# The combinations for the seven-product form: made in small steps on plain weight tiles, apart from the transposes

## Chip, core and metric

One core of a Trainium2 chip runs the whole kernel in one launch. The metric is device time in microseconds (us), the median of several executions.

## What is computed

A two-layer decoder trunk over 256 tokens of 2048 channels, float32. Layer 0 is a diagonal state-space mixer with a gated output, layer 1 an attention layer; each is followed by the same feed-forward block, which takes most of the time:

```python
def swiglu(u, w_gate, w_up, w_down):
    return (jax.nn.silu(u @ w_gate) * (u @ w_up)) @ w_down
...
u = rmsnorm(h, g_ffn[i])
h = h + swiglu(u, w_gate[i], w_up[i], w_down[i])      # D_MODEL 2048, D_FF 5632
```

## The kernel before

Every float32 operand of a matmul is split into a rounded part hi and a rest lo, and a product is three matmuls (hi by hi, lo by hi, hi by lo). The weights stream from HBM in tiles of 512 by 512, 1 MB each; a job is the use of one tile by TensorE (PE). `jobs` is a list, and the order of everything around it is written out by hand: `run_stream` (line 148) walks the list, and for job i it issues the matmuls, then the splits of the tiles ahead (`split_ahead`, line 121), then the functions that were hung behind job i (`j.after`, filled from `pend`). A split is `hi` on ScalarE (ACT, line 113) and `lo = raw - hi` on VectorE (DVE, line 114), in units of two blocks (128x1024); a full tile has two units. The hi and lo buffers hold four units, so a new split waits until PE has left the unit that it overwrites. DVE and ACT each work in the order of issue: what is hung behind job i stands in both queues between the split of job i+1 and that of job i+2.

A plain tile is 4 blocks by 2 token halves by 3 matmuls, 24 matmuls of 512 columns. The feed-forward block goes over D_FF in eleven groups of 512 columns, in two halves (groups 0 to 5, then 6 to 10); after each half comes the down product of that half. Groups after the first use a seven-product (Strassen-like) form for one 2x2 corner of the product: seven small tiles of 6 matmuls each and six plain tiles, 13 jobs in this order: small 1, 6, 7, plain, small 5, plain, small 2, 3, 4, and four plain tiles (jobs 9 to 12). Four of the small products need combinations of the weights (`S_T1` to `S_T4`, lines 786 to 789, on DVE; those for a group are made behind jobs 10 and 11 of the group before) and combinations of u. The down products use the same form, with combinations of g.

The combinations of u, `SC["c"]`, are made once per layer by `s_combine` (line 187). It stands in `u_chunk` (line 641) in the place of the transposing routine `hT_blocks` for the first 4 of 16 channel blocks: it transposes those blocks with PE, scales them, splits them, and forms, splits and stores the combinations, for two block pairs b = 0 and 1, all behind one job. In layer 0 this is a job of the gated output (the glu product), in layer 1 a job of the w_o product. The other 12 blocks go through `hT_blocks` (line 171) at later jobs.

The combinations of g, `SC["g"]`, are made once per half by `g_combine` (line 872). `g_rows` (line 858) transposes a finished group of g on PE into a PSUM bank `tr`, one token half a at a time, behind jobs 2 and 3 of the next group, splits it, and for the first two groups of a half calls `g_combine` at once: n = 0 (one copy) and n = 1 (copy, difference, split) in the second group, n = 2 (nothing) and n = 3 in the third. `g_combine` with n = 3 is one chain on DVE and ACT: five combining operations on DVE and three splits, each an ACT copy and a DVE subtraction, 128x512 each.

In the same group `s_evac` (line 813) empties the PSUM banks: behind job 9 two silus on ACT and one subtraction on DVE, behind job 12 four operations on DVE, which give the g that `g_rows` transposes in the next group.

Of the kernel before, what the change touches and what calls it, by code (L numbers as in the profile page):

```python
# [9 lines left out]
F32 = mybir.dt.float32  # L10
F32R = mybir.dt.float32r
AF = mybir.ActivationFunctionType
OP = mybir.AluOpType
# [17 lines left out]
def trunk_kernel(ctx: ExitStack, tc: tile.TileContext, par, x_tok, x_grp, b_st, g_st, c_st, cst, gvec,  # L31
# [24 lines left out]
    def bank(tag):  # L56
        return ps.tile([128, 512], F32, name=f"{tag}_{bank.n()}", tag=tag, bufs=2 if tag in ("tr", "x") else 1)
# [15 lines left out]
    def add(src, t, mm, after=None):  # L73
        j = Job()
        j.src, j.t, j.mm, j.after, j.pre = src, t, mm, after or [], []
        j.part, j.make, j.home = None, None, None
        jobs.append(j)
        return j
# [105 lines left out]

    SC = {}

    def s_combine(un, g):

        t = big.tile([128, 4096], F32R, name=f"sc_{un}", tag="DA"[un == "u_f1"])
        q = big.tile([128, 2, 2, 4, 128], F32R, name=f"sq_{un}", tag="Q")  # L190
        SC["c"] = t[:, 0:2048].rearrange("p (s n b t) -> p s n b t", s=2, n=4, b=2)
        SC["g"] = [q, t[:, 2048:4096].rearrange("p (s n b t) -> p s n b t", s=2, n=2, b=4)]
        SC["x"] = [big.tile([128, 512], F32, name=f"sx{n}_{un}", tag=f"X{n}") for n in range(2)]
        for b in range(2):
            tr = bank("tr").rearrange("p (b a t) -> p b a t", b=2, a=2)
            X = rows.tile([128, 2, 2, 128], F32, name=f"X{b}_{un}", tag="row")
            V = rows.tile([128, 4, 128], F32, name=f"V{b}_{un}", tag="row")
            for bb in range(2):
                for a in range(2):
                    k = b + 2 * bb  # L200
                    pe.transpose(tr[:, bb, a], h[:, a, 128 * k:128 * k + 128], ident)
            for bb in range(2):
                k = b + 2 * bb
                x = X[:, bb].rearrange("p a t -> p (a t)")
                act.activation(X[:, bb], tr[:, bb], AF.Copy, scale=g[:, k:k + 1])
                act.activation(uT[un][:, 0, k], x, AF.Copy)
                dve.tensor_tensor(uT[un][:, 1, k], x, uT[un][:, 0, k], op=OP.subtract)
            dve.tensor_tensor(V[:, 2], X[:, 0, 1], X[:, 0, 0], op=OP.subtract)
            dve.tensor_tensor(V[:, 0], X[:, 0, 1], X[:, 1, 1], op=OP.subtract)
            dve.tensor_tensor(V[:, 1], X[:, 1, 1], V[:, 2], op=OP.subtract)  # L210
            dve.tensor_tensor(V[:, 3], X[:, 1, 0], V[:, 1], op=OP.subtract)
            act.activation(SC["c"][:, 0, :, b], V, AF.Copy)
            dve.tensor_tensor(SC["c"][:, 1, :, b], V, SC["c"][:, 0, :, b], op=OP.subtract)


    pt = ring.tile([128, 32, 64], F32, name="gam", tag="hi")
# [409 lines left out]
    def row():  # L626
        return rows.tile([128, 512], F32, name=f"row{bank.n()}", tag="row")
# [13 lines left out]
    def u_chunk(j, c, name, gs):  # L641
        def f():
            if c == 0:
                u_tile(name)
            if c == 0 and name != "u_kv":
                s_combine(name, gv[:, gs])
            else:
                hT_blocks(range(4 * c, 4 * c + 4), uT[name], gv[:, gs])
        pend.append((j, f))

    PS = {}
# [105 lines left out]
    def gu_job(nm, un, own, kg, first, last, joins=None):  # L757
        o = opnd1(lambda: uT[un])

        def f(j):  # L760
            if joins is None and first:
                gu_acc(nm, own)
            mm3(acc[nm], o, 4 * kg, j, first, last, joins=joins or ())
        return f
# [93 lines left out]
    def g_rows(l, hf, c, src, a):  # L858
        def f():
            t = src()  # L860
            tr = bank(NT[a]).rearrange("p (b t) -> p b t", b=4)
            for b in range(4):
                pe.transpose(tr[:, b], t[:, 128 * b:128 * b + 128], ident)
            dst, b0 = g_at(l, hf, 4 * (c - PARTS[hf][0]))
            ts = slice(128 * a, 128 * a + 128)
            act.activation(dst[:, 0, b0:b0 + 4, ts], tr, AF.Copy)
            dve.tensor_tensor(dst[:, 1, b0:b0 + 4, ts], tr, dst[:, 0, b0:b0 + 4, ts], op=OP.subtract)
            if c - PARTS[hf][0] < 2:
                g_combine(2 * (c - PARTS[hf][0]) + a, tr, dst[:, :, b0:b0 + 4])
        return f  # L870

    def g_combine(n, tr, g):

        v4 = lambda t: t.rearrange("p (b t) -> p b t", b=4)
        X0, X1 = [v4(t) for t in SC["x"]]

        def put(i, src):
            d = SC["g"][i // 2]
            act.activation(d[:, 0, i % 2], src, AF.Copy)
            dve.tensor_tensor(d[:, 1, i % 2], src, d[:, 0, i % 2], op=OP.subtract)  # L880

        if n == 0:
            act.activation(X0, tr, AF.Copy)
        if n == 1:
            act.activation(X1, tr, AF.Copy)
            dve.tensor_tensor(X0, tr, X0, op=OP.subtract)
            put(2, X0)
        if n == 3:
            V = v4(row())
            dve.tensor_tensor(X1, X1, tr, op=OP.subtract)  # L890
            put(0, X1)
            dve.tensor_tensor(V, tr, X0, op=OP.subtract)
            put(1, V)
            t0 = slice(0, 128)
            dve.tensor_tensor(X0, g[:, 0, :, t0].bitcast(F32), V, op=OP.subtract)
            dve.tensor_tensor(X0, X0, g[:, 1, :, t0].bitcast(F32), op=OP.add)
            put(3, X0)


    def d_load(l, hf, cp, wd):  # L900
# [114 lines left out]
    def ffn(l, un, wg, wu, wd, r, down_evac):  # L1015
        for hf, (ca, cb) in enumerate(PARTS):
            for c in range(ca, cb):
                own = (c + 1) % 2
                j0 = len(jobs)
                if c == 0:  # L1020
                    for nm, w in (("gate", wg), ("up", wu)):
                        for kg in range(4):
                            add(w, 4 * c + kg, gu_job(nm, un, own, kg, kg == 0, kg == 3))
                    pend.append((j0 + 4, gate_evac(c, r)))
                    pend.append((j0 + 7, gu_end))
                    pend.append((j0 + 8, up_evac(c)))
                    src = lambda a, c=c: (lambda: sil[c][a])
                else:
                    pend.append((j0 - 5, s_load(l, c, wg, wu)))
                    pend.append((j0 - 3, S_T1))  # L1030
                    pend.append((j0 - 2, S_T2))
                    pend.append((j0 - 2, S_T3))
                    X = lambda nm, w, kg: add(w, 4 * c + kg, gu_job(nm, un, own, kg, kg == 1, kg == 3, (0,) if nm == "gate" else (0, 1)))
                    for i in (1, 6, 7):
                        s_add(i, un, own)
                    X("gate", wg, 1)
                    s_add(5, un, own)
                    X("gate", wg, 2)
                    for i in (2, 3, 4):
                        s_add(i, un, own)  # L1040
                    X("gate", wg, 3)
                    for kg in (1, 2, 3):
                        X("up", wu, kg)
                    for n in (0, 1, 2, 4, 9, 12):
                        pend.append((j0 + n, s_evac(n, c, r)))
                    src = lambda a, c=c: (lambda: gr[c, a])
                e = len(jobs) + (2 if c + 1 < cb else 0)
                for a in range(2):
                    pend.append((e + a, g_rows(l, hf, c, src(a), a)))
            k0, k1 = ca, cb  # L1050
            for cp in range(2):
                if l == 1 and hf == 1 and cp == 1:
                    for c in (2, 3):
                        for kg in range(k0, k1):
                            add(wd, 11 * c + kg, mm_job(("down", l, hf, c), kg == k0, kg == k1 - 1, g_opnd(l, hf), 4 * (kg - k0)))
                        chunk_end(len(jobs), down_evac(c))
                    continue
                down_pair(l, hf, cp, wd, (cp + hf + 1) % 2, r)
                n = len(jobs)
                for i in range(2):  # L1060
                    c = 2 * cp + i
                    if hf == 0:
                        chunk_end(n - 1 + i, lambda c=c: add_hr(("down", l, 0, c), c, r))
                    else:
                        chunk_end(n - 1 + i, down_evac(c))
                        if l == 0:
                            u_chunk(n + 1 + i, c, "u_kv", 0)
# [430 lines left out]
```

## Time and profile before

| | us |
|---|---|
| median of 3 executions | 2116.58 |
| lowest and highest | 2113.69, 2120.05 |
| the profiled execution, its own time | 2113.41 |
| its span in the trace | 2111.3 |
| PE busy in it | 2058.3 (97%) |
| DVE busy | 1548.0 (73%) |
| ACT busy | 1054.6 (50%) |
| POOL (GpSimd) busy | 150.9 (7%) |

The span is the time from the first to the last instruction in the trace. Busy shares are averages over the whole span; what ends a wait in a stretch is read from the timeline of that stretch. A matmul's recorded end is modelled and lies after the start of the next one, so the distance from start to start tells more of PE's pace than its busy time.

### The profile page before, as it was taken

Reading aid. Unit: us, or ns where it says so; the run is one execution under the profiler, and the core shown is the slowest. Engines: PE = TensorE matmul, PEld = TensorE weight load, DVE = VectorE, ACT = ScalarE, POOL = GpSimd, SP = SyncE. Lnnn points to the kernel's source line nnn. Section 1 sums busy time; section 2 is a strip of 40 time slices with the busy share of each in tenths; the row PEclk is TensorE's granted clock in tenths of the full one; section 3 lists DMA queues with packets and bytes.
Section 4 is the critical chain, followed back from the end, with each engine's and each line's share of the span. In section 5 each row is a group of like instructions: output and inputs, shape, how many; then the busy total and the mean of one; then the engine's idle time right before and its main releaser. Section 6 shows DMA issues by size and latency. Waiting matters only on the chain.

```text
span 2111.3 us, 28945 instructions
## 1 busy us (share of the span) xinstructions
PE 2058.3 (97%) x11508; PEld 1720.3 (81%) x11508; DVE 1548.0 (73%) x2124; ACT 1054.6 (50%) x1326; POOL 150.9 (7%) x105
## 2 busy tenths in 40 slices
PE   7999999999999999999999999999999999999998
PEld 6778787888888778888999998787788888778886
DVE  8984867777887777787555555667777878777784
ACT  6344555544554545555444444555455554544553
POOL 7741400000000000000000000000000000000010
PEclk9999999999999999999999999999999999999999
DMA  3035555555545455554544544555465456545544
GB/s 141 25 121 154 184 199 187 212 200 191 216 174 216 160 178 181 199 199 160 176 164 162 179 162 165 175 215 174 173 215 198 157 200 241 197 168 191 199 170 149
DMA packets 54055, 376.20 MB, mean 178 GB/s; under 512 B 6432, under 2 KB 6944, under 8 KB 9120
## 3 DMA queue, kind: packets, MB, share of 16 engines
q1 hardware_dynamic: 53920, 374.36, 49.7%
q8 instruction: 90, 1.47, 0.3%
q14 instruction: 45, 0.37, 0.1%
HBM read 370.14 MB, written 2.10 MB: 176 GB/s over the span
## 4 chain that ended last, share of the span: by engine, by line
PE 80%; DVE 12%; ACT 4%; issue 3%; DMA 0%; SPq 0%; ACTq 0%; POOL 0%; POOLq 0%; DVEq 0%
PE acc L139 12%; PE acc L138 12%; PE acc L137 12%; DVE lo L114 5%; PE tr L139 4%; PE tr L137 4%; PE tr L138 4%; PE x L138 3%; PE x L137 3%; PE x L139 3%; PE acc L1106 3%; PE acc L1107 3%; PE acc L1105 3%; ACT hi L113 3%; PE acc L146 2%
## 5 line engine op out<-in xcount | busy, mean ns | idle before, releaser
L114 DVE TENSOR_TENSOR lo<-raw,hi 128x1024 fp32r<-128x1024 f32 x552 | 666.9, 1242 | 202.8 <-ACT hi L113 199.3
L113 ACT ACTIVATE hi<-raw 128x1024 fp32r<-128x1024 f32 x566 | 575.9, 1053 | 200.0 <-PE acc L138 107.8
L137 PE MATMUL acc<-hi,u_f 128*128 128x512 f32 x608 | 238.0, 392 | 0.6 <-ACT hi L113 0.5
L139 PE MATMUL acc<-lo,u_f 128*128 128x512 f32 x608 | 237.2, 390 | 0.7 <-DVE lo L114 0.7
L138 PE MATMUL acc<-hi,u_f 128*128 128x512 f32 x608 | 237.0, 390 | 0.0
L139 PEld LDWEIGHTS acc<-lo,u_f 128*128 128x128 f32 x608 | 114.2, 188 | 25.4 <-DVE lo L114 1.6
L137 PEld LDWEIGHTS acc<-hi,u_f 128*128 128x128 f32 x608 | 114.2, 188 | 24.4 <-ACT hi L113 0.9
L138 PEld LDWEIGHTS acc<-hi,u_f 128*128 128x128 f32 x608 | 114.2, 188 | 23.8 <-DVE u_f L182 0.3
L113 ACT ACTIVATE hi<-st 128x1024 fp32r<-128x1024 f32 x60 | 63.3, 1056 | 115.2 <-DVE st L783 111.9
L139 PE MATMUL acc<-lo,g 128*128 128x512 f32 x256 | 99.9, 390 | 0.5 <-DVE lo L114 0.5
L137 PE MATMUL acc<-hi,g 128*128 128x512 f32 x256 | 100.0, 391 | 0.0
L138 PE MATMUL acc<-hi,g 128*128 128x512 f32 x256 | 99.7, 390 | 0.0
L137 PE MATMUL x<-hi,u_f 128*128 128x512 f32 x240 | 94.4, 393 | 0.0
L139 PE MATMUL x<-lo,u_f 128*128 128x512 f32 x240 | 93.6, 390 | 0.0
L138 PE MATMUL x<-hi,u_f 128*128 128x512 f32 x240 | 93.5, 390 | 0.0
L137 PE MATMUL tr<-hi,u_f 128*128 128x512 f32 x240 | 93.5, 389 | 0.0
L139 PE MATMUL tr<-lo,u_f 128*128 128x512 f32 x240 | 93.5, 389 | 0.0
L138 PE MATMUL tr<-hi,u_f 128*128 128x512 f32 x240 | 93.5, 389 | 0.0
L114 DVE TENSOR_TENSOR lo<-st,hi 128x1024 fp32r<-128x1024 f32 x60 | 73.3, 1222 | 25.6 <-ACT hi L113 24.1
L164 POOL TENSOR_TENSOR sml<-sml,half 128x2 f32<-128x2 f32 x4 | 2.8, 700 | 1121.7 <-DVE sml L163 1121.6
L1105 PE MATMUL acc<-uq,hi 128*128 128x256 f32 x256 | 74.0, 289 | 0.0
L1105 PE MATMUL acc<-u_kv,hi 128*128 128x256 f32 x256 | 73.3, 287 | 0.1
(375 smaller groups left out, 4806.4 us busy)
## 6 DMA issues: line engine op xcount, KB each, us to landing
raw<-w_gate SPq DMA_DIRECT2D x68, 1024.0 KB, 5.0
raw<-w_up SPq DMA_DIRECT2D x68, 1024.0 KB, 4.9
raw<-w_down SPq DMA_DIRECT2D x67, 1024.0 KB, 5.0
raw<-w_kv SPq DMA_DIRECT2D x32, 1024.0 KB, 4.9
su<-w_up SPq DMA_DIRECT2D x20, 1024.0 KB, 4.8
sg<-w_gate SPq DMA_DIRECT2D x20, 1024.0 KB, 7.1
raw<-w_glu SPq DMA_DIRECT2D x16, 1024.0 KB, 5.0
raw<-w_q SPq DMA_DIRECT2D x16, 1024.0 KB, 4.8
```

The source lines that it names most:

```text
L113: act.activation(hi, raw, AF.Copy)
L114: (pool if i < NPRE else dve).tensor_tensor(lo, raw, hi, op=OP.subtract)
L137: pe.matmul(pr, oh, j.hi[kb], start=first and kb == 0 and not jn, stop=False, skip_group_check=jn)
L138: pe.matmul(pr, ol, j.hi[kb], start=False, stop=False, skip_group_check=jn)
L139: pe.matmul(pr, oh, j.lo[kb], start=False, stop=last and kb == 3 and not jn, skip_group_check=jn)
L146: pe.matmul(pr, oh, j.lo[kb], start=False, stop=first and kb == n - 1, skip_group_check=join)
L164: pool.tensor_tensor(dst, tot, half, op=OP.pow)
L1105: pe.matmul(p, j.hi[kb][:, s], u[:, 0], start=first and kb == 0 and n % 2 == 0, stop=False)
L1106: pe.matmul(p, j.hi[kb][:, s], u[:, 1], start=False, stop=False)
L1107: pe.matmul(p, j.lo[kb][:, s], u[:, 0], start=False, stop=last and kb == 3 and n % 2 == 1)
```

## The change

`s_combine` no longer transposes. All 16 channel blocks now go through `hT_blocks`. A new function `s_tiles` takes the buffers behind job 1 of the first group of the layer's feed-forward block (8 plain tiles), and `s_combine(un, b)` runs for one block pair behind job 2 and for the other behind job 5. It builds its input by one new DVE addition, hi + lo of the split blocks; the combining operations are the same as before.

`g_rows` only remembers its PSUM bank in `gt_`. `g_combine` becomes six steps: n = 0, 1, 2 for the first group of a half, behind jobs 9, 10 and 11 of the group after it, and n = 3, 4, 5 for the second group, behind jobs 9, 10 and 11 of the group after that. The operations are the same, read from the same PSUM banks, which are thus held some seven jobs longer.

```diff
@@ -184,33 +184,25 @@
 
     SC = {}
 
-    def s_combine(un, g):
+    def s_tiles(un):
 
         t = big.tile([128, 4096], F32R, name=f"sc_{un}", tag="DA"[un == "u_f1"])
         q = big.tile([128, 2, 2, 4, 128], F32R, name=f"sq_{un}", tag="Q")
         SC["c"] = t[:, 0:2048].rearrange("p (s n b t) -> p s n b t", s=2, n=4, b=2)
         SC["g"] = [q, t[:, 2048:4096].rearrange("p (s n b t) -> p s n b t", s=2, n=2, b=4)]
         SC["x"] = [big.tile([128, 512], F32, name=f"sx{n}_{un}", tag=f"X{n}") for n in range(2)]
-        for b in range(2):
-            tr = bank("tr").rearrange("p (b a t) -> p b a t", b=2, a=2)
-            X = rows.tile([128, 2, 2, 128], F32, name=f"X{b}_{un}", tag="row")
-            V = rows.tile([128, 4, 128], F32, name=f"V{b}_{un}", tag="row")
-            for bb in range(2):
-                for a in range(2):
-                    k = b + 2 * bb
-                    pe.transpose(tr[:, bb, a], h[:, a, 128 * k:128 * k + 128], ident)
-            for bb in range(2):
-                k = b + 2 * bb
-                x = X[:, bb].rearrange("p a t -> p (a t)")
-                act.activation(X[:, bb], tr[:, bb], AF.Copy, scale=g[:, k:k + 1])
-                act.activation(uT[un][:, 0, k], x, AF.Copy)
-                dve.tensor_tensor(uT[un][:, 1, k], x, uT[un][:, 0, k], op=OP.subtract)
-            dve.tensor_tensor(V[:, 2], X[:, 0, 1], X[:, 0, 0], op=OP.subtract)
-            dve.tensor_tensor(V[:, 0], X[:, 0, 1], X[:, 1, 1], op=OP.subtract)
-            dve.tensor_tensor(V[:, 1], X[:, 1, 1], V[:, 2], op=OP.subtract)
-            dve.tensor_tensor(V[:, 3], X[:, 1, 0], V[:, 1], op=OP.subtract)
-            act.activation(SC["c"][:, 0, :, b], V, AF.Copy)
-            dve.tensor_tensor(SC["c"][:, 1, :, b], V, SC["c"][:, 0, :, b], op=OP.subtract)
+
+    def s_combine(un, b):
+        X = rows.tile([128, 2, 2, 128], F32, name=f"X{b}_{un}", tag="row")
+        V = rows.tile([128, 4, 128], F32, name=f"V{b}_{un}", tag="row")
+        hi, lo = [uT[un][:, n, b:b + 3:2].rearrange("p b (a t) -> p b a t", a=2).bitcast(F32) for n in range(2)]
+        dve.tensor_tensor(X, hi, lo, op=OP.add)
+        dve.tensor_tensor(V[:, 2], X[:, 0, 1], X[:, 0, 0], op=OP.subtract)
+        dve.tensor_tensor(V[:, 0], X[:, 0, 1], X[:, 1, 1], op=OP.subtract)
+        dve.tensor_tensor(V[:, 1], X[:, 1, 1], V[:, 2], op=OP.subtract)
+        dve.tensor_tensor(V[:, 3], X[:, 1, 0], V[:, 1], op=OP.subtract)
+        act.activation(SC["c"][:, 0, :, b], V, AF.Copy)
+        dve.tensor_tensor(SC["c"][:, 1, :, b], V, SC["c"][:, 0, :, b], op=OP.subtract)
 
 
     pt = ring.tile([128, 32, 64], F32, name="gam", tag="hi")
@@ -642,10 +634,7 @@
         def f():
             if c == 0:
                 u_tile(name)
-            if c == 0 and name != "u_kv":
-                s_combine(name, gv[:, gs])
-            else:
-                hT_blocks(range(4 * c, 4 * c + 4), uT[name], gv[:, gs])
+            hT_blocks(range(4 * c, 4 * c + 4), uT[name], gv[:, gs])
         pend.append((j, f))
 
     PS = {}
@@ -865,36 +854,43 @@
             ts = slice(128 * a, 128 * a + 128)
             act.activation(dst[:, 0, b0:b0 + 4, ts], tr, AF.Copy)
             dve.tensor_tensor(dst[:, 1, b0:b0 + 4, ts], tr, dst[:, 0, b0:b0 + 4, ts], op=OP.subtract)
-            if c - PARTS[hf][0] < 2:
-                g_combine(2 * (c - PARTS[hf][0]) + a, tr, dst[:, :, b0:b0 + 4])
-        return f
-
-    def g_combine(n, tr, g):
+            gt_[a] = tr
+        return f
+
+    gt_ = {}
+
+    def g_combine(n, l, hf):
 
         v4 = lambda t: t.rearrange("p (b t) -> p b t", b=4)
-        X0, X1 = [v4(t) for t in SC["x"]]
 
         def put(i, src):
             d = SC["g"][i // 2]
             act.activation(d[:, 0, i % 2], src, AF.Copy)
             dve.tensor_tensor(d[:, 1, i % 2], src, d[:, 0, i % 2], op=OP.subtract)
 
-        if n == 0:
-            act.activation(X0, tr, AF.Copy)
-        if n == 1:
-            act.activation(X1, tr, AF.Copy)
-            dve.tensor_tensor(X0, tr, X0, op=OP.subtract)
-            put(2, X0)
-        if n == 3:
-            V = v4(row())
-            dve.tensor_tensor(X1, X1, tr, op=OP.subtract)
-            put(0, X1)
-            dve.tensor_tensor(V, tr, X0, op=OP.subtract)
-            put(1, V)
-            t0 = slice(0, 128)
-            dve.tensor_tensor(X0, g[:, 0, :, t0].bitcast(F32), V, op=OP.subtract)
-            dve.tensor_tensor(X0, X0, g[:, 1, :, t0].bitcast(F32), op=OP.add)
-            put(3, X0)
+        def f():
+            X0, X1 = [v4(t) for t in SC["x"]]
+            if n == 0:
+                act.activation(X0, gt_[0], AF.Copy)
+            if n == 1:
+                act.activation(X1, gt_[1], AF.Copy)
+                dve.tensor_tensor(X0, gt_[1], X0, op=OP.subtract)
+            if n == 2:
+                put(2, X0)
+            if n == 3:
+                dve.tensor_tensor(X1, X1, gt_[1], op=OP.subtract)
+                put(0, X1)
+            if n == 4:
+                gt_["v"] = v4(row())
+                dve.tensor_tensor(gt_["v"], gt_[1], X0, op=OP.subtract)
+                put(1, gt_["v"])
+            if n == 5:
+                t0 = slice(0, 128)
+                g, b0 = g_at(l, hf, 4)
+                dve.tensor_tensor(X0, g[:, 0, b0:b0 + 4, t0].bitcast(F32), gt_["v"], op=OP.subtract)
+                dve.tensor_tensor(X0, X0, g[:, 1, b0:b0 + 4, t0].bitcast(F32), op=OP.add)
+                put(3, X0)
+        return f
 
 
     def d_load(l, hf, cp, wd):
@@ -1021,6 +1017,9 @@
                     for nm, w in (("gate", wg), ("up", wu)):
                         for kg in range(4):
                             add(w, 4 * c + kg, gu_job(nm, un, own, kg, kg == 0, kg == 3))
+                    pend.append((j0 + 1, lambda: s_tiles(un)))
+                    for b in range(2):
+                        pend.append((j0 + 2 + 3 * b, lambda b=b: s_combine(un, b)))
                     pend.append((j0 + 4, gate_evac(c, r)))
                     pend.append((j0 + 7, gu_end))
                     pend.append((j0 + 8, up_evac(c)))
@@ -1047,6 +1046,9 @@
                 e = len(jobs) + (2 if c + 1 < cb else 0)
                 for a in range(2):
                     pend.append((e + a, g_rows(l, hf, c, src(a), a)))
+                if c - ca < 2:
+                    for n in ((0, 1, 2), (3, 4, 5))[c - ca]:
+                        pend.append((e - 2 + 9 + n % 3, g_combine(n, l, hf)))
             k0, k1 = ca, cb
             for cp in range(2):
                 if l == 1 and hf == 1 and cp == 1:
```

## Rows read from the trace of the kernel before

**Rows 1.** The page, part 1: busy time of each engine, share, instructions.

```profile
PE 2058.3 (97%) x11508; PEld 1720.3 (81%) x11508; DVE 1548.0 (73%) x2124; ACT 1054.6 (50%) x1326; POOL 150.9 (7%) x105
```

**Rows 2.** Windows by group: stretch, length, busy PE, PEld, DVE, ACT, POOL; clock; DMA.

```profile
297.68:342.49 44.81, 43.73 (x195) 35.57 (x194) 33.20 (x34) 23.51 (x27) 0.00 (x0) 1.00 0.53 188
342.49:390.76 48.27, 45.68 (x196) 36.47 (x194) 37.67 (x41) 23.69 (x27) 0.00 (x0) 0.96 0.50 174
390.76:433.86 43.10, 43.10 (x195) 35.73 (x194) 33.27 (x34) 22.13 (x24) 0.00 (x0) 1.00 0.55 195
...
1468.96:1517.23 48.27, 44.54 (x195) 35.33 (x194) 37.67 (x41) 23.68 (x27) 0.00 (x0) 1.00 0.49 175
```

**Rows 3.** Timeline of PE: start, duration, instruction, [idle before, releaser].

```profile
361.40 0.50 PE L144 MATMUL acc<-hi,u_f 128*128 128x512 f32 x1 [1.49 <-ACT hi L113]
...
362.66 0.80 PE L146 MATMUL acc<-lo,u_f 128*128 128x512 f32 x1 [0.53 <-DVE lo L114]
```

**Rows 4.** Timeline of DVE in the same stretch.

```profile
354.35 0.68 DVE L890 TENSOR_TENSOR sx_u_f<-sx_u_f,tr 128x512 f32<-128x512 f32 x1
355.73 0.69 DVE L880 TENSOR_TENSOR sq_u_f<-sx_u_f,sq_u_f 128x512 fp32r<-128x512 f32 x1 [0.70 <-ACT sq_u_f L879]
...
360.43 0.69 DVE L880 TENSOR_TENSOR sc_u_f<-sx_u_f,sc_u_f 128x512 fp32r<-128x512 f32 x1 [0.69 <-ACT sc_u_f L879]
```

**Rows 5.** Timeline of DVE, jobs 10 to 12 of group 3 and the next start.

```profile
420.17 2.36 DVE L114 TENSOR_TENSOR lo<-raw,hi 128x1024 fp32r<-128x1024 f32 x2 [1.74 <-ACT hi L113]
422.45 1.22 DVE L783 TENSOR_TENSOR st<-sg,su 128x1024 f32<-128x1024 f32 x1
...
426.77 1.23 DVE L114 TENSOR_TENSOR lo<-sg,hi 128x1024 fp32r<-128x1024 f32 x1 [0.83 <-ACT hi L113]
427.91 1.22 DVE L783 TENSOR_TENSOR st<-st,su 128x1024 f32<-128x1024 f32 x1
...
433.40 0.68 DVE L817 TENSOR_TENSOR row<-tr,row 128x512 f32<-128x512 f32 x1
...
437.00 2.36 DVE L114 TENSOR_TENSOR lo<-raw,hi 128x1024 fp32r<-128x1024 f32 x2 [0.87 <-ACT hi L113]
```

**Rows 6.** Timeline of PE at the same start of a group.

```profile
438.85 0.40 PE L139 MATMUL acc<-lo,u_f 128*128 128x512 f32 x1
```

**Rows 7.** Windows as in rows 2, around the transposes of u.

```profile
226.32:243.23 16.91, 12.93 (x51) 9.81 (x50) 14.67 (x21) 10.69 (x20) 5.91 (x4) 0.90 0.40 136
244.02:255.51 11.49, 11.30 (x51) 8.98 (x50) 9.94 (x13) 7.28 (x13) 6.00 (x4) 1.00 0.51 178
256.30:268.90 12.60, 11.58 (x51) 8.91 (x50) 9.61 (x15) 6.72 (x13) 3.34 (x3) 1.00 0.49 164
...
1343.01:1384.27 41.26, 39.01 (x172) 31.50 (x171) 24.73 (x29) 21.17 (x29) 0.65 (x1) 1.00 0.58 193
1385.06:1390.62 5.56, 5.56 (x28) 4.55 (x26) 3.66 (x6) 3.52 (x6) 0.00 (x0) 1.00 0.05 21
```

**Rows 8.** Timelines of PE and DVE in the glu product.

```profile
235.69 0.50 PE L137 MATMUL acc<-hi,zT 128*128 128x512 f32 x1 [3.65 <-ACT hi L113]
...
225.13 2.52 DVE L678 TENSOR_TENSOR row<-row,zk 128x256 f32<-128x256 f32 x4
...
229.34 0.28 DVE L208 TENSOR_TENSOR V_u_f<-X_u_f 128x128 f32<-128x128 f32 x1
...
231.05 0.69 DVE L213 TENSOR_TENSOR sc_u_f<-V_u_f,sc_u_f 128x512 fp32r<-128x512 f32 x1 [0.70 <-ACT sc_u_f L212]
...
254.44 2.31 DVE L114 TENSOR_TENSOR lo<-raw,hi 128x1024 fp32r<-128x1024 f32 x1
```

**Rows 9.** Timelines of DVE, ACT and PE, jobs 3 and 4, layer 0.

```profile
272.48 0.48 DVE L182 SCALAR_TENSOR_TENSOR u_f<-tr,gv,u_f 128x256 fp32r<-128x256 f32 x1 [0.54 <-ACT u_f L181]
...
272.35 2.95 ACT L113 ACTIVATE hi<-raw 128x1024 fp32r<-128x1024 f32 x3
...
275.92 0.39 PE L137 MATMUL acc<-hi,u_f 128*128 128x512 f32 x1
```

## The prediction, made before the changed kernel ran

> **What bounds the kernel now.** I read the page's first part first. PE is busy 97% of the span and DVE 73% [rows 1]: the time is PE's, and a change to DVE and ACT work can only win where PE waits for them. The next view is the windows, cut from the first matmul of one group of the feed-forward block to the first of the next. A group that carries no combination lasts 43.10 us and PE is busy for all of it; the second group of a half, behind whose jobs 2 and 3 `g_combine` makes n = 0 and 1, lasts 44.81, and the third, with n = 3, 48.27 [rows 2]. That is 1.71 and 5.17 us lost, 6.88 per half. The windows of the other three halves repeat this pattern within 0.02 us, so the four halves lose 27.5 us at these places.
>
> Then the timeline says why. In the third group PE stops at a small tile, first for the ACT piece and then for the DVE piece of the weight split [rows 3]. At that time DVE is inside `g_combine`: the chain starts at 354.35 and ends at 361.12, 6.8 us in which three 0.7 us gaps wait for ACT's copy [rows 4], and the split of the next small tile stands behind it. A small tile feeds PE for a quarter of a plain one, so the splits there have no room for a 6.8 us chain. The chain is exposed there and a group without it has no stall at all, so the transposes themselves, which every group has, are not the cause.
>
> One figure has to be chosen with care. By PE's busy time the two groups lose 1.08 and 2.59 us (length less busy), 14.7 in four halves; the lengths say 27.5. A matmul's recorded end lies after the next one's start, so each stall looks shorter than it is; I take the lengths. The Trainium skill, "Perfetto Trace Analysis", section "Identifying the Most-Contended Engine", says the same of matmul busy time and asks for the weight-load busy share instead. By that (idle of 9.24 and 11.80 us against 7.37 in the group without a stall) [rows 2] the loss is 25.2; the trace's lengths decide for 27.5, and by the page's measure the total below would be 2.3 us less.
>
> In the third groups the clock reads 0.96, but in layer 1's it reads 1.00 and the length is the same 48.27 [rows 2]. The DVE queue, not the clock, sets that stall, and I count nothing more for the clock.
>
> **The u part, before.** In the glu product `s_combine` leaves PE waiting 3.65 us for one split [rows 8]. Two undisturbed jobs take at most 2 x 5.56 = 11.1 us [rows 7], so the window from 226.32 loses 5.8 us. The next two windows, which start after a plain `hT_blocks` and beside the same glu work, lose 0.4 and 1.5. In the w_o product PE idles 2.25 us in the window from 1343.01 (41.26 less 39.01) [rows 7]; I take 2.5, since idle again hides a bit.
>
> **What the change removes and adds.** No matmul is added or lost: the eight transposes go on as part of `hT_blocks`. DVE gains four additions of 128x512, each about 0.69 like its neighbours [rows 4]; ACT loses a few copies. No DMA moves.
>
> *g, first group of a half (n = 0, 1, 2).* Two ACT copies, a DVE subtraction and a split (ACT 0.63, DVE 0.69) go to jobs 9 to 11. The DVE queue there waits 0.83 us ahead of the split of `sg` [rows 5], and ACT is busy for only 22.13 of 43.10 us in a group [rows 2]. Step 1 pushes DVE by 0.6, which that gap takes; step 2 pushes `S_T2` and `S_T3` by 0.6, before gaps of about 0.1 and 0.7 at the next two splits. Cost 0; if that cover were gone, 1.3 us per half. The 1.71 goes.
>
> *g, second group (n = 3, 4, 5).* I walk the queue in a group that has nothing else, group 3 of layer 0, the fourth of its half [rows 5].
> - Step 3 behind job 9: DVE is idle 1.74 us and more ahead of 420.17; its 2 us fit. Cost 0.
> - Step 4: V could start at 422.45, where `S_T1` starts now; 0.68 for V, 0.70 wait for ACT, 0.61 to the next start. `S_T1` moves to 424.44. Also ACT's splits of job 12 wait for that copy, but they are needed only at the tile that starts 5.4 us before 433.86. The split of `sg` moves from 426.77 to 427.86.
> - Step 5: two DVE operations, the ACT copy, the rest: 429.00 to 431.79. `S_T2` moves from 427.91 to 431.71, `S_T3` to 432.85. The splits of the small tiles that need them end at 435.37 and 436.5; PE wants them at about 435.68 and 437.04. They just hold, by 0.3 and 0.5. (433.86 is where the group starts [rows 2]; a small tile is 6 matmuls, 1.36 us, a quarter of a plain one's 5.44.)
> - `s_evac` of job 12 moves from 433.40 to 436.43, and the next split behind it from 437.00 to 439.10, so its first unit ends at 440.3. PE wants that at 438.85 [rows 6]; this is the new late one: a stall of 1.45 us.
>
> So per half 6.88 goes and 1.45 comes. In four halves: 27.5 - 5.8 = 21.7. Ends for the new stall: 0, if a piece runs a little sooner than I chained it, and 4.0, if the walk is 1.5 us short, since then both small tiles stall too, each with a wait for ACT and one for DVE as in [rows 3]. I take 1.45, the walked value.
>
> By the Trainium skill, "VectorE: DVE Perf Modes", section "The DRAIN you can't avoid", the next operation starts only after the one before has left the pipe. The trace shows two splits in 2.36 us where one takes 1.23 [rows 5], so they overlap by 0.1; by the page's rule my ten hand-offs per half would add some 0.8 us each half, 3.2 in all.
>
> *u, transposes.* `hT_blocks` alternates between ACT and DVE; at the last call of layer 0, which nothing disturbs, DVE needs 2.9 us from about 270.06 to 272.96, and ACT is free 0.6 earlier [rows 9]. Behind the glu job DVE comes free at about 227.6 (225.13 + 2.52) [rows 8], so the call ends at 230.5, ACT's next split runs from 229.9 to 230.9, and lo follows at 232.2. PE, which starts 24 matmuls at 226.32 and needs 5.56 us for them [rows 7], wants hi at 231.9 and lo at 232.3: the loss of 5.8 goes to 0. But then the second call loses the pause that the first stall gave it. The glu chain (DVE sum, two POOL additions beside which a split takes 2.31 instead of 1.23 [rows 8], sigmoid, multiplication) then lies as it does in the third window, so I give it that one's loss: 0.4 becomes 1.4, and the third stays 1.5. Gain 5.8 - 1.0 = 4.8. Ends 3.0 (the chain moves the loss on) and 6.5. In the w_o product 2.5 goes to 0, as at the two calls later in the same layer, after which PE runs 24 matmuls in 5.56 without a wait [rows 7].
>
> *u, combinations.* One step is an addition (0.69), then four 128x128 operations and a wait for ACT (1.71 from the first of them to the start of the last subtraction, 229.34 to 231.05) [rows 8], and that subtraction (0.69): 3.1 us of DVE. In layer 0 the first lies behind job 2, right after the last `hT_blocks`. DVE is free there at 272.96 and ACT could go on at 272.35 [rows 9]; the step's ACT copy comes at 274.6, so ACT's next split starts at 275.2, hi comes at 276.2 and lo at 277.5. PE wants them at 275.92 and 276.4 [rows 9]: 0.3 + 0.9 = 1.2 us. The other three find slots where DVE runs two plain splits per 5.44 us tile, with 2 us or more spare: 0, or 1.2 each at the other end (3.6).
>
> **Sum.** 21.7 + 4.8 + 2.5 - 1.2 = 27.8 us. From the profiled execution's 2113.4 this gives 2085.6; that execution lies 3.2 below the median of the runs shown (2116.6), from which it gives 2088.8. A median is asked for, so I stay near the latter: 2088 us.
>
> **Rivals.**
> - *No new stall in the plain tiles* (the pieces interleave better than my walk, and step 2 and 4 hide wholly): gain 27.5 + 4.8 + 2.5 = 34.8, about 2080. For it: DVE is idle 9.8 us per group [rows 2]. Against: the walked lateness sits just where those gaps are small.
> - *The lateness reaches the small tiles*: 4.0 per half: 21.7 becomes 11.5, gain 17.6, about 2098. For it: margins of only 0.3 and 0.5 us. Against: the walk takes every ACT hand-over at 0.70 already.
> - *The chains are exposed where they land, and the kernel is slower.* Per half 6.8 us for n = 3 to 5 and 1.3 for n = 0 to 2, 32.4 in all, and 12.4 for four u steps, 44.8, against 27.5 + 5.8 + 2.5 = 35.8 removed: +9, about 2125. It decides from where jobs 9 to 12 have no idle DVE time left. Against: 9.8 us idle per group against 8.1 us of chain.
> - *It doesn't do what it says*: the stall belongs to `g_rows` and the small tiles and comes back there, time unchanged, 2116. Against: groups with `g_rows` and without `g_combine` have none [rows 2].
>
> **How the numbers follow.** Forecast 0.57; no new stall 0.18; small tiles reached 0.19; exposed 0.03; nothing 0.03. The range runs from the second case's time less 1 to the third's plus 2 for the spread of the runs: 2079 to 2100. About 0.3% (6 us) can be told from no change in this kernel. Faster by more: the first three cases, 0.94; within: 0.03; slower: 0.03.
>
> **What would show it.** In the profile after: second groups of 43.1 us; third groups of 43.1 us with no DVE gap over small tiles 2, 3 and 4; fourth groups of about 44.6 us with PE waiting for DVE's lo at the first plain tile; in the glu product no wait above 1 us after the first transposes, but about 1.4 us after the second; one wait of about 1.2 us at job 4 of layer 0's first group. Wrong would be: fourth groups of 47 us, or PE waiting at small tiles for `st` or `su`, or third groups still above 45.

## The result

| | us |
|---|---|
| before, median of 4 executions | 2117.03 (2113.69 to 2120.05) |
| changed, median of 4 executions | 2087.64 (2086.84 to 2088.84) |
| ratio, with its 95% interval | 0.9862 (0.9845 to 0.9879) |
| the changed kernel's profiled execution, and its span | 2087.43, 2085.7 |

The kernel is 1.4% faster. By the medians it gained 29.4 us, by the two profiled executions 26.0; that difference is taken up behind the experiments.

The page after, parts 1 and 4, shows the same matmuls and almost the same DVE time:

```profile
PE 2046.5 (98%) x11508; PEld 1717.5 (82%) x11508; DVE 1549.8 (74%) x2128; ACT 1052.6 (50%) x1318; POOL 150.9 (7%) x105
...
PE 79%; DVE 4%; ACT 2%; issue 2%; ACTq 0%; POOLq 0%; POOL 0%; DVEq 0%
```

Against [rows 1] DVE does four instructions more and ACT eight fewer; the four are the new additions. No engine does less work worth speaking of. What went is time in which PE waited; PE's busy time fell with it, by 11.8 us for the same matmuls, since matmuls behind a wait are recorded longer (0.80 us in [rows 3], 0.40 in [rows 6]).

The windows after, with the columns of [rows 2]: the second, third and fourth group of layer 0's first half, and the fourth group of its second half.

```profile
294.87:338.00 43.13, 43.13 (x196) 35.70 (x195) 33.24 (x34) 23.62 (x27) 0.00 (x0) 1.00 0.54 195
338.00:381.10 43.10, 43.10 (x196) 35.70 (x195) 34.75 (x38) 22.64 (x26) 0.00 (x0) 1.00 0.55 195
381.10:425.88 44.78, 43.44 (x196) 35.53 (x195) 36.18 (x37) 23.43 (x26) 0.00 (x0) 1.00 0.52 188
...
767.26:812.04 44.78, 43.44 (x196) 35.54 (x195) 36.18 (x37) 23.55 (x26) 0.00 (x0) 1.00 0.52 188
```

These answer [rows 2]. The second group went from 44.81 to 43.13 and the third from 48.27 to 43.10, the length of a group without a stall. The fourth group, which had none, went from 43.10 to 44.78. That pattern stands in all four halves.

The timeline of DVE in the third group after, from job 10 on, and of PE at the start of the fourth:

```profile
369.69 0.68 DVE L885 TENSOR_TENSOR row<-tr,sx_u_f 128x512 f32<-128x512 f32 x1
...
371.67 1.22 DVE L772 TENSOR_TENSOR st<-sg,su 128x1024 f32<-128x1024 f32 x1
...
375.08 1.22 DVE L114 TENSOR_TENSOR lo<-sg,hi 128x1024 fp32r<-128x1024 f32 x1
376.21 0.69 DVE L890 TENSOR_TENSOR sx_u_f<-g,row 128x512 f32<-128x512 f32 x1
...
378.94 1.22 DVE L772 TENSOR_TENSOR st<-st,su 128x1024 f32<-128x1024 f32 x1
...
383.70 0.69 DVE L806 TENSOR_TENSOR row<-acc,row 128x512 f32<-128x512 f32 x1
...
386.35 2.35 DVE L114 TENSOR_TENSOR lo<-raw,hi 128x1024 fp32r<-128x1024 f32 x2
```

```profile
385.89 0.40 PE L138 MATMUL x<-hi,u_f 128*128 128x512 f32 x1
387.62 0.50 PE L139 MATMUL x<-lo,u_f 128*128 128x512 f32 x1 [1.34 <-DVE lo L114]
387.96 0.40 PE L137 MATMUL x<-hi,u_f 128*128 128x512 f32 x1
388.20 0.39 PE L138 MATMUL x<-hi,u_f 128*128 128x512 f32 x1
```

This is [rows 5] and [rows 6] again with steps 4 and 5 in between: V and its split ahead of `S_T1` (371.67), the split of `sg` behind it, step 5 ahead of `S_T2` (378.94), and at the end of the queue the split (386.35) for which PE stops at 387.62.

Around the transposes of u, after: the three glu windows that answer [rows 7], the rest of layer 0's first group, and the w_o window.

```profile
226.86:237.91 11.05, 11.05 (x51) 8.97 (x50) 9.50 (x11) 7.28 (x13) 5.71 (x4) 1.00 0.60 208
238.70:251.32 12.62, 11.60 (x52) 8.90 (x50) 11.07 (x15) 7.36 (x14) 6.03 (x4) 1.00 0.48 164
252.11:264.71 12.60, 11.59 (x52) 8.90 (x51) 9.60 (x15) 6.72 (x13) 3.35 (x3) 1.00 0.49 162
265.87:294.87 29.00, 28.23 (x121) 22.47 (x121) 23.11 (x31) 16.02 (x19) 0.00 (x0) 1.00 0.66 247
...
1331.03:1369.26 38.23, 38.23 (x172) 31.60 (x171) 21.47 (x24) 18.72 (x26) 0.65 (x1) 1.00 0.61 209
```

The first glu window fell from 16.91 to 11.05. The second rose from 11.49 to 12.62, and the third kept 12.60. The w_o window, the same 172 matmuls, fell from 41.26 to 38.23: 3.0 us, where the idle time read 2.25.

The fourth window has no row ahead of the prediction; in the kernel before, the same stretch was this:

```profile
270.06:297.68 27.62, 27.60 (x120) 22.64 (x121) 18.91 (x19) 15.09 (x17) 0.00 (x0) 1.00 0.68 260
```

It grew by 1.38 us. That is the price of the first u step behind job 2.

### The profile page after: what moved, and what is told of

It reads as the page before. It is cut to its first block, busy times and chain, and to the rows that moved or that the text cites. A ratio compares the mean times of both kernels' runs of the same rounds, so it can differ in the third digit from the quotient of the medians.

```text
span 2085.7 us, 28934 instructions
## 1 busy us (share of the span) xinstructions
PE 2046.5 (98%) x11508; PEld 1717.5 (82%) x11508; DVE 1549.8 (74%) x2128; ACT 1052.6 (50%) x1318; POOL 150.9 (7%) x105
## 4 chain that ended last, share of the span: by engine, by line
PE 79%; DVE 4%; ACT 2%; issue 2%; ACTq 0%; POOLq 0%; POOL 0%; DVEq 0%
PE acc L139 11%; PE acc L137 11%; PE acc L138 11%; PE x L139 3%; PE tr L137 3%; PE tr L139 3%; PE tr L138 3%; PE x L137 3%; PE x L138 3%; PE acc L1108 3%; PE acc L1109 3%; PE acc L1107 3%; DVE lo L114 2%; PE acc L146 2%; PE acc L144 2%; PE acc L145 2%
```

## The experiments

Each kernel below starts from the changed one. "Less" and "more" without a reference are against the kernel before, which ran beside them: its median was 2116.12 us beside the first four (12 executions) and 2114.39 beside the last four (9). The changed kernel itself ran only beside the 2117.03.

**Do the two parts add up?** The first kernel keeps the g part and puts back `s_combine` with its transposes, the second keeps the u part and puts back `g_combine` inside `g_rows`.

```diff
 e1: s_combine, u_chunk as before
-                    pend.append((j0 + 1, lambda: s_tiles(un)))
-                    for b in range(2):
-                        pend.append((j0 + 2 + 3 * b, lambda b=b: s_combine(un, b)))
 e2: g_rows, g_combine as before
-                    for n in ((0, 1, 2), (3, 4, 5))[c - ca]:
-                        pend.append((e - 2 + 9 + n % 3, g_combine(n, l, hf)))
```

> Only the g part of the change; s_combine stays as in the kernel before. Theory (the terms of the sum add up): third groups at 43.1 us, fourth groups about 44.7, the glu and w_o windows as before (16.9 us and 2.25 us idle). 4 x 6.88 goes, 4 x 1.6 comes: 21 us less than the kernel before, about 2096. Rival (the two parts share a cause, such as a DVE queue that runs late from the glu product on): much less than 21 us, or stalls left in the third groups.

Measured: 2092.43 us against 2116.12 before, ratio 0.9887 (0.9872 to 0.9902), 23.7 us less by the medians; its profiled execution, at 2091.59, is 21.8 below the profiled one of before.

> Only the u part; g_combine stays as in the kernel before. Theory: the glu windows lose 1.6, 1.6 and about 1.4 us where they lost 5.8, 0.4 and 1.5, the w_o stall goes, job 4 of layer 0's first group waits 1.4 us; third groups stay at 48.27. About 6 us less than the kernel before, about 2111. Rival (shared cause): third groups get shorter too, gain over 10 us.

Measured: 2110.46 us, ratio 0.9973 (0.9963 to 0.9983), 5.7 us less. The two ratios multiply to 0.9860, and the whole change has 0.9862. The parts are separate, and four fifths of the gain are the g part's. The rival, a shared cause, falls: the third groups of the second kernel last 48.3 us like those of the kernel before, but for one, which is taken up below. The first glu window of this kernel lost nothing (11.08 us), where 1.6 was expected.

**Is it the small steps or the place?** The change does two things to the g chain: it cuts it into steps, and it moves it from jobs 2 and 3, beside small tiles, to jobs 9 to 11, plain tiles. One kernel does only the move (all steps in one piece behind job 9), one only the cutting (steps behind jobs 3, 4 and 5).

```diff
-                        pend.append((e - 2 + 9 + n % 3, g_combine(n, l, hf)))
+                        pend.append((e - 2 + 9, g_combine(n, l, hf)))            # e4
+                        pend.append((e - 2 + 3 + n % 3, g_combine(n, l, hf)))    # e5
```

> As the changed kernel, but all three steps of g stand behind job 9, one chain of 6.8 us again, at a plain tile. Theory (the place decides, since DVE and ACT are idle there while PE works on a plain tile): third groups 43.1 plus about 1.3 us at job 11, whose splits come late, fourth groups near 43.1: within 3 us of the changed kernel, 2085 to 2090. Rival (the small steps decide): the unbroken chain stalls PE as it did before, 4 to 5 us per half, 2100 or more.

Measured: 2085.88 us, ratio 0.9859 (0.9842 to 0.9876): the time of the changed kernel. Its third and fourth group:

```profile
337.12:381.66 44.54, 43.70 (x196) 35.55 (x194) 37.46 (x41) 23.81 (x27) 0.00 (x0) 1.00 0.53 189
381.66:424.76 43.10, 43.10 (x195) 35.71 (x194) 33.46 (x34) 22.13 (x24) 0.00 (x0) 1.00 0.54 195
```

Its DVE and PE in the third group:

```profile
360.67 0.68 DVE L881 TENSOR_TENSOR sx_u_f<-sx_u_f,tr 128x512 f32<-128x512 f32 x1
...
366.76 0.69 DVE L869 TENSOR_TENSOR sc_u_f<-sx_u_f,sc_u_f 128x512 fp32r<-128x512 f32 x1 [0.70 <-ACT sc_u_f L868]
367.37 0.68 DVE L806 TENSOR_TENSOR row<-acc,row 128x512 f32<-128x512 f32 x1
369.80 2.36 DVE L114 TENSOR_TENSOR lo<-raw,hi 128x1024 fp32r<-128x1024 f32 x2 [1.74 <-ACT hi L113]
```

```profile
369.81 0.50 PE L137 MATMUL acc<-hi,u_f 128*128 128x512 f32 x1 [0.31 <-ACT hi L113]
...
371.07 0.50 PE L139 MATMUL acc<-lo,u_f 128*128 128x512 f32 x1 [0.53 <-DVE lo L114]
```

The chain stands unbroken, 6.8 us from 360.67 to 367.45, as in [rows 4]. Behind jobs 2 and 3 such a chain cost 5.17 us; here the group loses 1.44 (44.54 less 43.10), at the start of job 11, where PE waits at 369.81 for `hi`, and at 371.07 for the split on DVE that waited 1.74 for the same `hi` (ACT is the late one: its splits start only at 368.72, behind a silu that needs the subtraction which DVE makes after the chain, at 367.37), and the fourth group loses nothing. The place alone brings the whole gain of the g part.

> As the changed kernel, but the three steps of g stand behind jobs 3, 4 and 5, in small steps beside the small tiles. Theory (the place decides): the splits of small tiles 2, 3, 4 and of the plain tile behind them come late, 5 to 6 us per half in the third group, fourth groups at 43.1: the gain of the g part is gone, about 2103 to 2112. Rival (the small steps decide): as the changed kernel or within 5 us of it, 2083 to 2093.

Measured: 2108.03 us, ratio 0.9962 (0.9946 to 0.9977), 8.1 less. That is little more than the u part by itself brings. One of its second groups and three of its four third groups, then its PE at the last small tile (line 144 is the first matmul of each of its two blocks) and the plain tile behind it (lines 137 to 139):

```profile
297.42:340.60 43.18, 43.18 (x195) 35.70 (x194) 33.07 (x34) 23.28 (x27) 0.00 (x0) 1.00 0.55 195
340.60:391.45 50.85, 47.44 (x195) 37.30 (x194) 37.76 (x41) 23.68 (x27) 0.00 (x0) 0.93 0.47 166
732.95:782.28 49.33, 45.91 (x195) 36.24 (x194) 37.77 (x41) 23.68 (x27) 0.00 (x0) 0.97 0.48 171
...
1465.43:1515.43 50.00, 46.84 (x195) 36.72 (x194) 37.76 (x41) 23.68 (x27) 0.00 (x0) 0.93 0.47 169
```

```profile
362.10 0.50 PE L144 MATMUL acc<-hi,u_f 128*128 128x512 f32 x1 [1.10 <-ACT hi L113]
...
363.69 0.40 PE L144 MATMUL acc<-hi,u_f 128*128 128x512 f32 x1
363.93 0.39 PE L145 MATMUL acc<-hi,u_f 128*128 128x512 f32 x1
...
366.29 0.79 PE L137 MATMUL acc<-hi,u_f 128*128 128x512 f32 x1 [1.74 <-ACT hi L113]
...
368.14 0.63 PE L137 MATMUL acc<-hi,u_f 128*128 128x512 f32 x1
368.57 0.63 PE L138 MATMUL acc<-hi,u_f 128*128 128x512 f32 x1
```

The third groups lose 6.2 to 7.75 us where the old chain lost 5.17 and 5 to 6 was expected: cut into three and put behind jobs 3, 4 and 5, the steps hold up the splits of the last small tile and of the plain tile behind it, in part worse, because the clock drops (below). So for the long chain the cutting neither is needed (the fourth kernel) nor helps (the fifth). The words of the change name two things, and for the large loss only "plain weight tiles" does the work.

The short chain is another case. With n = 0, 1 and 2 behind jobs 3, 4 and 5 the four second groups last 43.13 to 43.18, where the old place, jobs 2 and 3 in one go, took 44.8. So this chain fits beside the small tiles too; whether by its steps or by the later jobs, no run separates. The 6.6 us that it saves nearly make up for the 7.1 that the third groups lose more than before.

**Are the waits that are left the ones named?** The changed kernel lost 1.68 in each fourth group, 1.38 at job 4 of layer 0 and 1.5 in each of two glu windows. Three kernels each move one thing to where the queue has room, and one does all three.

```diff
-                        pend.append((e - 2 + 9 + n % 3, g_combine(n, l, hf)))
+                        pend.append((e - 2 + (22 if n == 5 else 9 + n % 3), g_combine(n, l, hf)))   # e3
-                        pend.append((j0 + 2 + 3 * b, lambda b=b: s_combine(un, b)))
+                        pend.append((j0 + 3 + 3 * b, lambda b=b: s_combine(un, b)))                 # e6
-        u_chunk(len(jobs) - 4 + 2 * c, c, "u_f0", 2)
+        u_chunk(len(jobs) - 4 + (0, 1, 3, 6)[c], c, "u_f0", 2)                                      # e7
```

> As the changed kernel, but the last step of g (n = 5) waits 11 jobs longer: behind job 9 of the fourth group instead of behind job 11 of the third, where the weight sums S_T2 and S_T3 stand too. Theory (the stall of 1.6 us at the first plain tile of the fourth group is the lateness that step 5 adds to those sums): the stall goes in all four halves and none comes, 6.5 us less than the changed kernel, about 2081. Rival (it is due to step 4, or to the banks held longer): the stall stays at over 0.8 us.

Measured: 2080.52 us, ratio 0.9837 (0.9823 to 0.985). Step 5 is now behind job 9 of the fourth group, no longer ahead of `S_T2` and `S_T3`. The third and the fourth group:

```profile
339.65:382.75 43.10, 43.10 (x195) 35.70 (x194) 35.40 (x38) 23.29 (x26) 0.00 (x0) 1.00 0.55 195
382.75:425.85 43.10, 43.10 (x195) 35.70 (x194) 35.60 (x37) 22.77 (x25) 0.00 (x0) 1.00 0.55 195
```

The fourth group lost its 1.68: step 5, late ahead of `S_T2`, was the cause.

> As the changed kernel, but the two steps of u stand one job later, behind jobs 3 and 6 of the first group. Theory (the 1.4 us at job 4 of layer 0 come from the step standing right behind the last transposes): that wait goes, 1.4 us less, about 2086. Rival (the step costs the same anywhere in the group): no change, the wait moves to job 5.

Measured: 2085.7 us, ratio 0.9859 (0.9846 to 0.9873). By the medians alone one could not tell it from the changed kernel; the window can. The rest of layer 0's first group is back at its old length:

```profile
267.05:294.67 27.62, 27.61 (x121) 22.63 (x121) 20.84 (x29) 15.34 (x19) 0.00 (x0) 1.00 0.69 259
```

> As the changed kernel, but in layer 0 the second, third and fourth set of transposes stand behind jobs 13, 15 and 18 of the glu product instead of 14, 16 and 18, so that they no longer share a job with the glu multiplication. Theory (the second set loses 1.6 us only because the multiplication and the transposes stand together in DVE's queue): 2.5 to 3 us less than the changed kernel, about 2085. Rival (DVE and POOL are simply full in the glu product): the waits move to jobs 14 and 16 and the time stays.

Measured: 2084.93 us, ratio 0.9857 (0.9843 to 0.987). The glu windows, cut at its own calls of `hT_blocks`:

```profile
227.10:232.66 5.56, 5.56 (x27) 4.55 (x26) 4.01 (x6) 3.55 (x7) 2.34 (x2) 1.00 0.63 222
233.45:245.03 11.58, 11.34 (x51) 8.97 (x50) 10.03 (x15) 7.64 (x14) 5.39 (x4) 1.00 0.53 180
246.45:263.12 16.67, 16.67 (x75) 13.47 (x74) 14.00 (x19) 9.82 (x16) 6.73 (x5) 1.00 0.53 179
```

They hold one, two and three jobs. A job takes at most 5.56, so they lose 0, 0.5 and 0 (PE is busy for the whole of the first and the third). The transposes between the second and the third take 1.42 us instead of 0.79 (252.11 less 251.32 in the changed kernel), as PE waits there for POOL's `h`: 0.6 more. Together that is 1.1, where the changed kernel lost 1.5 twice: 1.9 less, not the 2.5 to 3 expected. So part of that loss was where the call stood against the glu chain, as the prediction had it.

> The three moves together: last step of g 11 jobs later, steps of u one job later, transposes away from the glu multiplication. Theory (the waits are separate): 6.5 + 1.4 + 2.7 = 10.6 us less than the changed kernel, about 2077, 40 us less than the kernel before. Rival (a stall that is removed uncovers another): 4 us less or under.

Measured: 2076.76 us, ratio 0.9819 (0.9805 to 0.9832). It beats both kernels, 37.6 us below the one before. Page, part 1, and its third and fourth group:

```profile
PE 2044.7 (98%) x11508; PEld 1718.9 (83%) x11508; DVE 1548.8 (75%) x2128; ACT 1053.0 (51%) x1318; POOL 150.7 (7%) x105
```

```profile
337.06:380.16 43.10, 43.10 (x195) 35.70 (x194) 35.40 (x38) 23.30 (x26) 0.00 (x0) 1.00 0.55 195
380.16:423.27 43.11, 43.11 (x196) 35.70 (x194) 35.62 (x37) 22.77 (x25) 0.00 (x0) 1.00 0.54 195
```

The work is the same as in [rows 1], down to 0.1% of DVE's time. The groups run at the length of a group with no combination in it; the combinations now cost nothing there. The longest waits of PE that are left, 4.5, 3.6 and 3.2 us, do not touch them.

**Executions set on one footing.** The opening of the kernel, which none of these edits touches, does not take the same time in each profiled execution. A fixed mark, behind most of it, is the first addition of the scan over `Z`, on DVE's timeline, here of the kernel before and of the last one:

```profile
37.90 0.23 DVE L594 TENSOR_TENSOR acc<-Z,acc 128x64 f32<-128x64 f32 x1 [0.45 <-ACT Z L406]
```

```profile
40.45 0.23 DVE L586 TENSOR_TENSOR acc<-Z,acc 128x64 f32<-128x64 f32 x1 [0.60 <-ACT Z L398]
```

From that mark to the end of the span:

| kernel | span | mark | rest | against before | against changed |
|---|---|---|---|---|---|
| before | 2111.3 | 37.90 | 2073.4 | | |
| changed | 2085.7 | 38.35 | 2047.4 | -26.0 | |
| g only (e1) | 2089.8 | 38.03 | 2051.8 | -21.6 | |
| u only (e2) | 2110.0 | 40.12 | 2069.9 | -3.5 | |
| one piece, plain tiles (e4) | 2082.3 | 38.65 | 2043.7 | | -3.7 |
| steps, small tiles (e5) | 2109.3 | 40.58 | 2068.7 | -4.7 | |
| step 5 late (e3) | 2080.6 | 39.68 | 2040.9 | | -6.4 |
| u step later (e6) | 2085.5 | 39.41 | 2046.1 | | -1.3 |
| other calls for u (e7) | 2082.5 | 38.39 | 2044.1 | | -3.2 |
| all three (e8) | 2076.5 | 40.45 | 2036.1 | -37.3 | -11.3 |

Part of these differences lies where none of the edits reaches. Two stretches hold the same matmuls in every kernel and yet differ between the profiled executions. One is a run of 22 matmuls of the opening, behind the mark; here it is in the changed and the one-piece kernel:

```profile
53.16:56.09 2.93, 2.93 (x22) 2.03 (x21) 2.93 (x9) 1.06 (x1) 2.85 (x3) 0.53 0.00 0
```

```profile
53.49:55.20 1.71, 1.71 (x22) 1.26 (x21) 1.71 (x7) 1.07 (x1) 1.71 (x2) 0.97 0.00 0
```

The other, in layer 1, goes from the first transposes for `u_kv` to the first matmul of lines 137 to 139 that reads it; here it is in the kernel before and the changed one:

```profile
978.18:1008.10 29.92, 27.42 (x224) 26.37 (x222) 17.19 (x26) 13.92 (x24) 0.69 (x1) 1.00 0.36 123
```

```profile
964.87:996.11 31.24, 28.74 (x223) 27.69 (x222) 17.19 (x26) 13.94 (x24) 0.69 (x1) 0.95 0.36 120
```

The matmuls of a pair are the same; what differs is the granted clock. The first stretch takes 1.71 us in e1 and e4 and 2.8 to 3.1 in the other eight. The second takes 31.2 to 31.4 at clock 0.95 in the changed kernel, e2, e3, e5 and e6, and 29.9 at 1.00 in the kernel before, e1, e4, e7 and e8.

With this the table closes. The three edits give 6.4, 1.3 and 3.2, and together 11.3; but 1.3 of the 3.2 and of the 11.3 is the layer-1 stretch, and the rest, 10.0, is the sum of the windows, 6.7, 1.4 and 1.9: separate causes. The one-piece kernel's 3.7 are 1.0 in its groups (0.24 in each half), 1.3 in layer 1 and 1.2 in the opening, to 0.2. The u part alone shows 3.5, but it lost 1.4 in layer 1 and 1.6 in one third group (below): 6.5 without them. And the 26.0 of the whole change would be 27.3 if the changed kernel's layer-1 stretch had run as it did in the kernel before.

## Why the prediction was right, point by point

*The old loss.* 6.88 per half was to go. The second and third groups went to 43.13 and 43.10. Right, also for the groups of n = 0, 1 and 2, costed at nothing because of the 0.83 gap and the free ACT.

*Steps 3 to 5.* The walk can be laid beside the trace after by shifting it 52.76 us earlier. `S_T2` was to start at 378.95 and did at 378.94; `s_evac` at 383.67, measured 383.70; the split behind it 386.34, measured 386.35; PE's late matmul 387.54, measured 387.62, so 1.53 behind its old place (386.09) where 1.45 was walked. By the lengths the stall costs 1.68. The step that is off is the one that counts only PE's waiting: the first matmul behind the wait is also followed later than usual, 0.34 from 387.62 to the next where the following ones are 0.23 apart. In four halves 6.7 against 5.8. With step 5 moved away the group has its 43.10 again, so nothing else is in it. The walk's margins of 0.3 and 0.5 at the small tiles held; the rival in which they don't did not come. Nor did the one without a new stall, nor the 0.8 us per half that hand-offs without overlap would have added.

*g part.* 27.5 - 6.7 = 20.8 by the windows, 21.7 predicted; the kernel with the g part alone measured 21.6 from the mark, 1.1 of it in the opening stretch (2.79 before, 1.71 there).

*Transposes of u.* The first glu window lost 5.8 and now loses 0 (11.05); the second went from 0.4 to 1.5, predicted 1.4; the third stayed at 1.5. Net 4.7, predicted 4.8. In the w_o product 3.0 went, predicted 2.5: idle did hide a bit, and more than the 0.25 that was added for it. The combination behind job 2 cost 1.38, predicted 1.2; the later three cost nothing, as in the term's lower end.

*Sum.* 20.8 + 4.7 + 3.0 - 1.4 = 27.1 us by the windows, 27.8 predicted. The sum was 0.7 us too large: 0.9 at the starts of the fourth groups and 0.3 in the two terms of u, less the 0.5 that the w_o product gave on top. From the mark it is 26.0; the layer-1 stretch, which ran 1.3 longer at the lower clock, makes up the difference to 0.2, and the sum had no term for it.

*The base.* From the profiled execution's own time, the sum gave 2085.6, and the profiled execution after took 2087.43, so that sum was 1.8 off, about what the terms (0.7) and the layer-1 stretch (1.3) make. The forecast of 2088.0 met the median of 2087.64 because it was set from the median: two errors that went against each other. Meeting it to 0.4 us is luck, since the medians of the kernel before differ by up to 2.6 us between the occasions (2117.03, 2116.12, 2114.39). The profiled execution of before lay 3.6 below its median, that of after 0.2 below its own, which is the 3.4 between 29.4 and 26.0. Three things are seen to vary: the opening, by 2.7 us between the marks above and by 1.2 behind them, the layer-1 stretch, by 1.3, and the price of a stall, next. How the 3.4 divides among them was not measured; the kernel before, with more stalls, also has times that spread more than those of the changed one (6.4 us against 2.0).

*The sentence on the clock was too strong.* "The DVE queue, not the clock, sets that stall, and I count nothing more for the clock": in the four halves before it held, 48.27 or 48.28 at 0.96 in three of them and at 1.00 in one [rows 2]. In the kernel with the u part alone, whose third groups are the same, the fourth half's is different:

```profile
1857.82:1907.73 49.91, 46.18 (x195) 36.45 (x194) 37.68 (x41) 23.69 (x27) 0.00 (x0) 0.97 0.47 169
```

It lost 1.64 more for the same queue. And in the kernel with the g part alone the first glu window, in which PE waits 3.66 us for the same split as in [rows 8], is 1.0 longer than in [rows 7]:

```profile
225.34:243.28 17.94, 14.24 (x52) 10.73 (x51) 15.71 (x24) 10.69 (x20) 5.99 (x5) 0.81 0.36 129
```

This one cost nothing in the end: the next two windows are 0.5 us shorter each than in [rows 7] (11.00 and 12.09). The 1.64 of the third group stayed, and so did the 1.3 in layer 1.

*Rivals.* A slower kernel by exposed chains would have needed plain tiles without room; the unbroken chain of the fourth kernel cost 1.44 there against 5.17 beside small tiles. "It doesn't do what it says" is out by the lengths of the groups.

## What to carry to other kernels

Where one engine bounds the kernel and another prepares its operands in a queue, look for the stretch in which the operands last longer than their preparation takes, and put side work there; in this kernel that was worth some 21 us, and cutting the long chain into steps was worth nothing. Then walk the queue behind the new place up to the next operation that somebody needs: here step 5 cost 1.68 us each time only because `S_T2` stood behind it, and one job number took that away. Measure a stall by the length of equal stretches that hold the same matmuls, compare profiled executions from a mark behind the part that varies, and before a remainder is put down to an edit, look at stretches that the edit does not reach: here one of them alone made 1.3 us.

## What the runs showed of the hardware

The same delay of a queue does not always cost PE the same. After a wait the matmuls can run on at half rate: in the fifth kernel above they start 0.24 us apart at 363.69, ahead of the wait of 1.74, and still 0.43 apart at 368.14, some 2 us behind it, in a group whose granted clock is 0.93 (1.00 is 2.4 GHz; half rate is the 1.2 GHz level). With the same stall, seven third groups of eight last 48.3 and one 49.91, the glu window 16.91 and 17.94, and the layer-1 stretch 29.9 in five profiled executions and 31.2 to 31.4 in the other five. What decides it in a given execution was not found.
